# Elementwise products moved from POOL to VectorE, column blocks side by side, and gate weights loaded early, in a two-block layer stack

## The chip, the cores and the metric

The kernel runs on one core of a Trainium2 chip. The metric is device time in microseconds (us) of one launch; before the change the median of three runs is 3601.03 us (3599.94 to 3604.13). TensorE is called PE here, VectorE DVE, ScalarE ACT, GpSimd POOL and SyncE SP.

## What the reference computes

All arithmetic is float32, on 256 tokens of width 2048, batch 1. The first block has two layers. Layer 0 (`e_`) projects the normed input to 6144 columns; one half of the mixer is HGRN2, a gated linear recurrence in chunks, the other a causal convolution and an RG-LRU recurrence; both are gated and go through `e_w_out`. Layer 1 (`o_`) projects to 8208 columns: 2048 of q and k (convolution, SiLU), 2048 each of v, output gate and z, and 8 + 8 gate columns at the end (8192 to 8207) that make the decay of an mLSTM; then `o_w_out`. Each layer ends with

```python
h = h + mix
pl = rmsnorm(p[i] @ ple_w[i], ple_norm[i])
h = h + sigmoid(h @ ple_gate_w[i]) * pl
```

The second block has two equal layers: an SSD mixer beside a latent attention (MLA) from one projection of 3664 columns, joined by `w_out`; cross attention to a memory of 256 rows; a SwiGLU of width 5632 (`w_gate`, `w_up`, `w_down`). Every product with a weight is a matrix product of 256 tokens.

## The kernel before

**Dense products.** A weight is read once. `wload` (L204) brings a piece of 2 x 128 rows and up to 512 columns into one of four `raw` buffers by DMA on SP's queue, ACT rounds it to `whi` (L217), DVE makes the rest `wlo = raw - whi` (L218). An input is split the same way (`split`, L293), and a product is hi x hi + hi x lo + lo x hi. `tokens_chunks` (L238) makes a block of up to 512 output columns for all tokens in two accumulators (of five), piece by piece over the input's features; `cols_chunks` (L256) puts the output's columns on partitions and takes four. A piece of `tokens_chunks` is 12 matmuls.

**Order.** PE's order is written out by hand. `Flow` (L58) holds a queue `dense` of pieces, each with a condition (its input features exist), and a heap of generators for the side work. A generator yields the number of us of PE work that should pass before it goes on; `mm` (L138) counts that work. So `yield 6.5` in `hgrn_mix` places the next level's products 6.5 counted us later in PE's order. The order on DVE, ACT, POOL and SP is a scheduler's, from its own costs and priorities; each engine then runs its list in order. Weight pieces have a high priority.

**Where the change lies.** `hgrn_mix` (L602) runs seven levels for each of two halves: DVE makes `qd` (L618) and updates `sf` (L630), POOL makes `kd = k * sf` (L625) and updates `pf` (L634, its tile is called `sg` in the trace), PE multiplies `kd` and `qd`, DVE copies the result under a mask into `pa` and `pb` (L650). The mask keeps only the products that come from the first half of each pair of blocks of `m` columns. `lru_mix` (L723) multiplies `gi` by `xc` on POOL (L745) on the way to a scan; the scan's result, gated and split, is the last of the four feature blocks of `e_w_out`. `softmax` (L1111) ends with a scaling of each part on POOL (L1126), 32 times for `pu` of MLA and 16 times for `xp` of the cross attention. In the SSD mixer POOL makes `xdt` (L1411), scales `xtm` (L1414) and multiplies the decays `e` by `cbm` (L1435). The decays are made on DVE by L1426 and L1430.

`mix_out` (L799) makes a layer's output product in four column blocks, one after the other; with `halves=True` (the second block's `w_out`) the first two are taken side by side: half the pieces of block 0, half of block 1, the rest of 0, the rest of 1. `swiglu` (L1651) works through the 11 hidden blocks in groups of 3, 3, 3 and 2; after each group's gate and up products it makes four down blocks over the group's features. `bc_scores` (L1189) makes `cbm` 13 counted us after the convolution that gives `xbcc` was issued. The gate columns of `o_w_in` are loaded with 256 columns of v, as two DMAs for each of eight pieces (L210, L1059).

Of the kernel before, what the change touches and what calls it, by code (L numbers as in the profile page):

```python
# [20 lines left out]
KT = 16  # L21
# [71 lines left out]
def _body(tc, a, cst, msk, out):  # L93
# [3 lines left out]
    with ExitStack() as ctx:  # L97
# [103 lines left out]
            V.memset(mh, -0.5)  # L201


        def wload(w, k0, nk, *segs):  # L204
            with hp():
                nn = sum(n for _, n in segs)
                raw = raw_p.tile([128, 2, 512], F32, tag="raw", name="raw")[:, :nk, :nn]
                at = 0
                for n0, n in segs:
                    nc.sync.dma_start(  # L210
                        raw[:, :, at:at + n],
                        w[k0 * 128:(k0 + nk) * 128, n0:n0 + n].rearrange("(k p) n -> p k n", p=128),
                    )
                    at += n
                hi = hl_p.tile([128, 2, 512], F32R, tag="hi", name="whi")[:, :nk, :nn]
                lo = hl_p.tile([128, 2, 512], F32R, tag="lo", name="wlo")[:, :nk, :nn]
                S.activation(hi, raw, AF.Copy)  # L217
                V.tensor_tensor(lo, raw, hi.bitcast(F32), ALU.subtract)  # L218
            return [(k0 + j, hi[:, j, :], lo[:, j, :]) for j in range(nk)]
# [382 lines left out]
        def hgrn_mix(hf, st_):  # L602
# [10 lines left out]
            for n, m in enumerate(HGRN_LEVELS + (128,)):  # L613
# [7 lines left out]
                if m == 1:  # L621
                    kd = k
                elif m < 128:
                    kd = kds[n % 2]
                    G.tensor_tensor(kd, k, sf, ALU.mult)  # L625
                else:
                    kd = kds[n % 2]
                    V.tensor_tensor(kd[:, :, 0:128], k[:, :, 0:128], sf[:, :, 0:128], ALU.mult)
                if m < 128:
                    V.tensor_tensor(  # L630
                        halves(sf)[:, :, 0, :], halves(sf)[:, :, 0, :],
                        halves(pf)[:, :, 1, m - 1:m].to_broadcast([128, 512 // m, m]), ALU.mult,
                    )
                    G.tensor_tensor(  # L634
                        halves(pf)[:, :, 1, :], halves(pf)[:, :, 1, :],
                        halves(pf)[:, :, 0, m - 1:m].to_broadcast([128, 512 // m, m]), ALU.mult,
                    )
                    yield 6.5
                    sc = mx_tile([128, 4, 2, 64])
                    with hp():  # L640
                        for j in range(4):
                            for st in range(2):
                                mm(
                                    sc[:, j, st, :], kd[:, j, st * 128:(st + 1) * 128],
                                    qd[:, j * 128 + st * 64:j * 128 + (st + 1) * 64], start=True, stop=True,
                                )
                    mask = mk[:, n * 64:(n + 1) * 64].rearrange("p (b m) -> p b m", m=m)
                    for st in range(2):
                        dst = pa[:, :, 0:128] if st == 0 else pb
                        V.copy_predicated(  # L650
                            dst.rearrange("p j (b two m) -> p j b two m", two=2, m=m)[:, :, :, 1, :],
                            mask.unsqueeze(1).to_broadcast([128, 4, 64 // m, m]),
                            sc[:, :, st, :].rearrange("p j (b m) -> p j b m", m=m),
                        )
                else:
                    yield 6.0
                    sc = mx_tile([128, 4, 128])
                    with hp():
                        for j in range(4):
                            mm(sc[:, j, :], kd[:, j, 0:128], qd[:, j * 128:(j + 1) * 128], start=True, stop=True)  # L660
                    S.copy(pa[:, :, 128:256], sc)
# [61 lines left out]
        def lru_mix(hf, xb):  # L723
# [18 lines left out]
                        S.activation(dst[:, q, :], gp[:, j, :], AF.Sigmoid, bias=vc(bias, hf * 4 + q))  # L742
            for q in range(4):
                S.activation(th[:, q, :], th[:, q, :], AF.Tanh, scale=sp4[:, hf * 4 + q:hf * 4 + q + 1])
            G.tensor_tensor(gi, gi, xc, ALU.mult)  # L745
            rec = xb
            V.tensor_scalar(rec, th, 1.0, None, ALU.add)
            for q in range(4):
# [34 lines left out]
        def load_rest():  # L783
# [7 lines left out]
                yield from block2_cols(l)  # L791
            load(pos_i, a["positions_2"][0].rearrange("(m p) -> p m", p=128))

        def stat(st, key="ss"):
            if key not in st:
                st[key] = small([128, 2, 4], key)
            return st[key]

        def mix_out(yp, ks, w, gain, pairs, st=None, between=None, halves=False):  # L799
            def done(c):  # L800
                def go(ps):
                    res_add(ps, c)
# [3 lines left out]
            for c in range(4):  # L806
                if c == 2 and between is not None:
                    between()
                if halves and c == 0:
                    two = [tokens_chunks(done(n), reader(yp), ks, w, n * 512, 512) for n in range(2)]  # L810
                    half = len(two[0]) // 2
                    flow.dense.extend(two[0][:half] + two[1][:half] + two[0][half:] + two[1][half:])
                elif not halves or c > 1:
                    tokens_by_cols(done(c), reader(yp), ks, w, c * 512, 512)

        hgrn_values()
# [3 lines left out]
        for hf in range(2):  # L820
            hgrn_out(hf)
            lru_out(hf)

        def out_and_ple(i, yp, ks, w, after, hook=None):
            pairs, pl, made = [], [], []
            at(lambda: flow.spawn(made[0], 1.0))
            mix_out(yp, ks, w, None, pairs, between=lambda: made.append(ple(i, pl)))
            if hook is not None:
                at(hook)
            ple_gate(i, pairs, pl, after)  # L830
# [280 lines left out]
        def softmax(parts, scale, nm):  # L1111
# [11 lines left out]
                )  # L1123
            V.reciprocal(sums[:, :n], sums[:, :n])
            for i, (dst, _) in enumerate(parts):
                G.tensor_scalar(dst, dst, sums[:, i:i + 1], 0.0, ALU.mult, ALU.add)  # L1126


        def mixers(l, x, sx, yy):
# [57 lines left out]
                flow.spawn(bc_scores(conv_act(evac_rbc(ps, sx["rbc"], "xbc"), 2)))  # L1187

            def bc_scores(bc):  # L1189
                yield 13.0  # L1190
                cbm = b["cbm"] = unit([128, 2, 384], "cbm")
                for g in range(2):
                    sc = mx_tile([128, 384])
# [201 lines left out]
            def ssd_inputs(g):  # L1395
# [9 lines left out]
                for m in range(2):  # L1405
                    def per_head(ap):
# [1 line left out]

                    gs = slice(g * 8, g * 8 + 8)
                    xv = xtm[:, m, :].rearrange("p (a b) -> p a b", a=8)  # L1410
                    G.tensor_tensor(  # L1411
                        xdt[:, m, :].rearrange("p (a b) -> p a b", a=8), xv, per_head(b["dt"][:, m, gs]), ALU.mult
                    )
                    G.tensor_tensor(xv, xv, per_head(mixcol[l][:, 2, gs]), ALU.mult)  # L1414
                yssd[g], xdts[g] = xtm, xdt

            def ssd_decay(g, pr):
# [14 lines left out]
                        ALU.subtract, ALU.max,  # L1432
                    )
                S.activation(e, e, AF.Exp, scale=-1.0)
                G.tensor_tensor(e, e, b["cbm"][:, g, :].unsqueeze(1).to_broadcast([128, 2, 384]), ALU.mult)  # L1435

            def ssd_pair(g, pr):
                e = es.pop((g, pr))
# [212 lines left out]
        def swiglu(l, x, sx, x_next, s_next):  # L1651
            for c0, c1 in ((0, 3), (3, 6), (6, 9), (9, 11)):
# [29 lines left out]
                for c in range(c0, c1):  # L1682
                    cols_by_tokens(got_gate, reader(x), K16, a["w_gate_2"][l], c * 512)
                    cols_by_tokens(got_up(c), reader(x), K16, a["w_up_2"][l], c * 512)
                for c in range(4):
                    tokens_by_cols(
                        got_down(c), reader(acts), list(range(c0 * 4, c1 * 4)), a["w_down_2"][l], c * 512, 512
                    )

        xs, ss = x2, s2  # L1690
        for l in range(2):
            yy, x3, s3, oo, x4, s4, x5, s5 = [None] * 4, [], {}, [], [], {}, [], {}
            mixers(l, xs, ss, yy)
            mix_out(yy, K16[8:] + K16[:8], a["w_out_2"][l], lambda i, l=l: vc(f"xn{l}", i), x3, s3, halves=True)
            cross(l, x3, s3, oo)
            mix_out(oo, [0, 1, 2, 3], a["w_xo_2"][l], lambda i, l=l: vc(f"ffn{l}", i), x4, s4)
            swiglu(l, x4, s4, x5, s5)
# [30 lines left out]
```

## Time and profile before

| | before |
|---|---|
| median of 3 runs | 3601.03 us |
| profiled execution, span | 3601.81 us, 3600.0 us |
| PE busy | 3493.4 us (97%), 17927 matmuls |
| DVE busy | 2233.1 us (62%) |
| ACT busy | 1787.6 us (50%) |
| POOL busy | 180.9 us (5%) |
| HBM read | 624.92 MB, 174 GB/s over the span |
| mean granted clock of PE | 0.983 |

Durations come from one profiled execution. "Idle before" in a row is the time for which the engine stood still ahead of that group, and the arrow names what ended it. A granted clock of 1.00 is 2.4 GHz, 0.50 is 1.2 GHz.

### The profile page before, as it was taken

Reading aid. Unit: us, or ns where it says so; the run is one execution under the profiler, and the core shown is the slowest. Engines: PE = TensorE matmul, PEld = TensorE weight load, DVE = VectorE, ACT = ScalarE, POOL = GpSimd, SP = SyncE. Lnnn points to the kernel's source line nnn. Section 1 sums busy time; section 2 is a strip of 40 time slices with the busy share of each in tenths; the row PEclk is TensorE's granted clock in tenths of the full one; section 3 lists DMA queues with packets and bytes.
Section 4 is the critical chain, followed back from the end, with each engine's and each line's share of the span. In section 5 each row is a group of like instructions: output and inputs, shape, how many; then the busy total and the mean of one; then the engine's idle time right before and its main releaser. Section 6 shows DMA issues by size and latency. Waiting matters only on the chain.

```text
span 3600.0 us, 46977 instructions
## 1 busy us (share of the span) xinstructions
PE 3493.4 (97%) x17927; PEld 2976.8 (83%) x17927; DVE 2233.1 (62%) x3070; ACT 1787.6 (50%) x2626; POOL 180.9 (5%) x181
## 2 busy tenths in 40 slices
PE   9999898999999998999999999999989999999999
PEld 7888787888888877888888888898778888888887
DVE  5778756655567666556656555567666565555555
ACT  5344454544446545565444444455456654444443
POOL 0212000000000012000000000000110000000000
PEclk9999999999999999999999999999999999999999
DMA  7445468788666653546666666565436565666665
GB/s 222 146 141 173 158 183 142 190 177 173 206 199 174 180 147 109 196 154 183 193 187 187 192 187 190 175 182 167 128 118 201 156 189 192 187 191 188 187 189 163
DMA packets 338658, 630.14 MB, mean 175 GB/s; under 512 B 24416, under 2 KB 48128, under 8 KB 338432
## 3 DMA queue, kind: packets, MB, share of 16 engines
q1 hardware_dynamic: 335472, 621.86, 59.3%
q10 hardware_dynamic: 2960, 5.29, 0.5%
q8 instruction: 140, 2.29, 0.3%
q14 instruction: 86, 0.70, 0.1%
HBM read 624.92 MB, written 2.14 MB: 174 GB/s over the span
## 4 chain that ended last, share of the span: by engine, by line
PE 79%; DVE 2%; ACT 1%; issue 1%; DMA 0%; POOL 0%; ACTq 0%; POOLq 0%; DVEq 0%
PE acc L143 74%; PE mx L143 3%; PE tr L147 2%; DVE wlo L218 0%; ACT whi L217 0%; DVE e L1426 0%; DVE e L1430 0%; DVE xbcc L406 0%; ACT L1121 0%; ACT L1183 0%; ACT junk L326 0%; DMA lb<-lanes 0%; DVE thl L296 0%; ACT xbcc L1183 0%; ACT pu L1121 0%
## 5 line engine op out<-in xcount | busy, mean ns | idle before, releaser
L218 DVE TENSOR_TENSOR wlo<-raw,whi 128x1024 fp32r<-128x1024 f32 (+2 forms) x1184 | 1426.1, 1206 | 1180.3 <-ACT whi L217 1170.0
L217 ACT ACTIVATE whi<-raw 128x1024 fp32r<-128x1024 f32 (+2 forms) x1184 | 1232.9, 1042 | 1572.7 <-PE acc L143 1486.0
L143 PE MATMUL acc<-whi,thl 128*128 128x512 f32 (+4 forms) x5440 | 1688.4, 387 | 20.0 <-ACT thl L295 15.6
L143 PE MATMUL acc<-thl,whi 128*128 128x512 f32 x3968 | 1410.5, 400 | 13.8 <-ACT v L883 8.7
L143 PEld LDWEIGHTS acc<-whi,thl 128*128 128x128 f32 x5440 | 1022.1, 190 | 217.8 <-ACT thl L295 16.8
L143 PE MATMUL acc<-thl,wlo 128*128 128x256 f32 x3968 | 1116.5, 281 | 0.7 <-DVE wlo L218 0.7
L143 PE MATMUL acc<-wlo,thl 128*128 128x512 f32 (+4 forms) x2720 | 1045.0, 384 | 3.8 <-DVE wlo L218 3.7
L143 PEld LDWEIGHTS acc<-thl,whi 128*128 128x128 f32 x3968 | 748.7, 189 | 193.6 <-ACT v L883 9.0
L143 PEld LDWEIGHTS acc<-thl,wlo 128*128 128x128 f32 x3968 | 753.3, 190 | 1.7 <-DVE wlo L218 1.0
L143 PEld LDWEIGHTS acc<-wlo,thl 128*128 128x128 f32 x2720 | 516.2, 190 | 96.5 <-DVE wlo L218 5.5
L298 ACT ACTIVATE thl<-tr,vcols 128x256 fp32r<-128x256 f32 x216 | 92.4, 467 | 50.2 <-DVE thl L299 46.8
L299 DVE SCALAR_TENSOR_TENSOR thl<-tr,vcols,thl 128x256 fp32r<-128x256 f32 x216 | 96.4, 477 | 8.5 <-ACT thl L298 6.5
L331 POOL TENSOR_TENSOR r<-rsq,mh 128x2 f32<-128x2 f32 x11 | 7.7, 697 | 1500.7 <-DVE rsq L330 1500.7
L357 DVE TENSOR_TENSOR h<-acc,h 128x512 f32<-128x512 f32 x112 | 72.4, 681 | 8.2 <-PE acc L143 8.1
L326 ACT ACTIVATE junk<-h 128x512 bf16<-128x512 f32 x72 | 44.9, 624 | 7.8 <-DMA h<-in_x 3.8
L147 PE MATMUL tr<-cc,h 128*128 128x128 f32 x320 | 42.4, 276 | 0.0
L147 PEld LDWEIGHTS tr<-cc,h 128*128 128x128 f32 x320 | 38.1, 143 | 4.7
L367 ACT COPY gg<-acc 128x256 f32<-128x256 f32 x88 | 31.9, 363 | 11.8 <-PE acc L143 11.8
L367 ACT COPY uu<-acc 128x256 f32<-128x256 f32 x88 | 31.9, 363 | 11.8 <-PE acc L143 11.8
L143 PE MATMUL mx<-xdt,e 128*128 128x64 f32 x192 | 26.1, 291 | 7.9 <-DVE thl L296 7.9
L143 PEld LDWEIGHTS mx<-xdt,e 128*128 128x128 f32 x192 | 25.6, 209 | 9.6 <-issue 9.1
L368 DVE TENSOR_TENSOR uu<-acc,uu 128x256 f32<-128x256 f32 x88 | 32.9, 415 | 0.0
(393 smaller groups left out, 1757.7 us busy)
## 6 DMA issues: line engine op xcount, KB each, us to landing
raw<-in_w_gate SPq DMA_DIRECT2D x176, 512.0 KB
raw<-in_w_up SPq DMA_DIRECT2D x176, 512.0 KB
raw<-in_w_down SPq DMA_DIRECT2D x176, 512.0 KB
raw<-in_o_w_in SPq DMA_DIRECT2D x120, 512.0 KB
raw<-in_e_w_in SPq DMA_DIRECT2D x96, 512.0 KB
raw<-in_w_in SPq DMA_DIRECT2D x80, 512.0 KB
raw<-in_ple_gate_w SPq DMA_DIRECT2D x64, 512.0 KB
raw<-in_w_out SPq DMA_DIRECT2D x64, 512.0 KB
```

The costliest lines, as they stand in the source:

```text
L143: PE.matmul(o, lhsT, rhs, start=start, stop=stop)
L147: PE.transpose(o, x, eye)
L217: S.activation(hi, raw, AF.Copy)
L218: V.tensor_tensor(lo, raw, hi.bitcast(F32), ALU.subtract)
L298: S.activation(hi, src, AF.Copy, scale=gain)
L299: V.scalar_tensor_tensor(lo, src, gain, hi.bitcast(F32), ALU.mult, ALU.subtract)
L326: S.activation(junk[:, :n], src, AF.Square, accum_out=dst)
L331: G.tensor_tensor(dst, tmp[:, :n], mh[:, :n], ALU.pow)
L357: V.tensor_tensor(hs, ps[m], hs, ALU.add)
L367: S.copy(u[:, q, :], ps[q][:, 0])
L368: V.tensor_tensor(u[:, q, :], ps[q][:, 1], u[:, q, :], ALU.add)
```

## The change

Products on POOL become DVE instructions; `kd` is made only for the half that the mask keeps from the third level (m = 8) on. `mix_out` takes `parts` in place of `halves`: with `(4, 6)` blocks 0 and 1 go side by side in runs of four, two and two pieces. It now holds for `e_w_out` and `o_w_out` too, and `swiglu` puts its first two down blocks side by side, all but the last two pieces of each first. The 16 gate columns are loaded by one DMA into `gw`, a tile of the `w` pool, ahead of `e_w_out`; `wload` copies them from there on DVE. Two yields change.

```diff
 def wload(w, k0, nk, *segs):
 ...
             for n0, n in segs:
+                if n0 in kept:
+                    V.tensor_copy(raw[:, :, at:at + n], kept[n0][:, k0:k0 + nk, :])
+                    at += n
+                    continue
                 nc.sync.dma_start(
 ...
 # hgrn_mix
-                    G.tensor_tensor(kd, k, sf, ALU.mult)
+                    if n < 3:
+                        V.tensor_tensor(kd, k, sf, ALU.mult)
+                    else:
+                        V.tensor_tensor(
+                            halves(kd)[:, :, 0, :], halves(k)[:, :, 0, :], halves(sf)[:, :, 0, :], ALU.mult
+                        )
 ...
-                    G.tensor_tensor(
+                    V.tensor_tensor(
                         halves(pf)[:, :, 1, :], halves(pf)[:, :, 1, :],
                         halves(pf)[:, :, 0, m - 1:m].to_broadcast([128, 512 // m, m]), ALU.mult,
                     )
-                    yield 6.5
+                    yield 7.0
 # lru_mix
-            G.tensor_tensor(gi, gi, xc, ALU.mult)
+            V.tensor_tensor(gi, gi, xc, ALU.mult)
 ...
+        def side_by_side(jobs, parts):
+            for i, j in zip((0,) + parts, parts + (len(jobs[0]),)):
+                for job in jobs:
+                    flow.dense.extend(job[i:j])
 # mix_out
-                if halves and c == 0:
-                    two = [tokens_chunks(done(n), reader(yp), ks, w, n * 512, 512) for n in range(2)]
-                    half = len(two[0]) // 2
-                    flow.dense.extend(two[0][:half] + two[1][:half] + two[0][half:] + two[1][half:])
-                elif not halves or c > 1:
+                if parts and c == 0:
+                    side_by_side([tokens_chunks(done(n), reader(yp), ks, w, n * 512, 512) for n in range(2)], parts)
+                elif not parts or c > 1:
                     tokens_by_cols(done(c), reader(yp), ks, w, c * 512, 512)
 ...
+        def keep_gates():
+            kept[8192] = wtile([128, KT, 16], "gw")
+            load(kept[8192], a["o_w_in"][0][:, 8192:8208].rearrange("(k p) n -> p k n", p=128))
 # out_and_ple
+            if i == 0:
+                at(keep_gates)
-            mix_out(yp, ks, w, None, pairs, between=lambda: made.append(ple(i, pl)))
+            mix_out(yp, ks, w, None, pairs, between=lambda: made.append(ple(i, pl)), parts=(4, 6))
 # softmax
-                G.tensor_scalar(dst, dst, sums[:, i:i + 1], 0.0, ALU.mult, ALU.add)
+                V.tensor_scalar(dst, dst, sums[:, i:i + 1], 0.0, ALU.mult, ALU.add)
 # bc_scores
-                yield 13.0
+                yield 20.0
 # ssd_inputs, ssd_decay: xdt (L1411), xtm (L1414) and e (L1435)
-                    G.tensor_tensor(
+                    V.tensor_tensor(
 ...
 # swiglu
-                for c in range(4):
-                    tokens_by_cols(
-                        got_down(c), reader(acts), list(range(c0 * 4, c1 * 4)), a["w_down_2"][l], c * 512, 512
-                    )
+                down = [
+                    tokens_chunks(got_down(c), reader(acts), list(range(c0 * 4, c1 * 4)), a["w_down_2"][l], c * 512, 512)
+                    for c in range(4)
+                ]
+                side_by_side(down[:2], (len(down[0]) - 2,))
+                for job in down[2:]:
+                    flow.dense.extend(job)
 # the second block's w_out
-            mix_out(yy, K16[8:] + K16[:8], a["w_out_2"][l], lambda i, l=l: vc(f"xn{l}", i), x3, s3, halves=True)
+            mix_out(yy, K16[8:] + K16[:8], a["w_out_2"][l], lambda i, l=l: vc(f"xn{l}", i), x3, s3, parts=(4, 6))
```

## Rows read from the trace of the kernel before

**Rows 1.** PE's waits by releaser: total us, times, longest.

```profile
PE tr L147 <- POOL pu L1126: 17.3, 2, 8.7
PE acc L143 <- ACT thl L295: 15.6, 3, 11.4
PE mx L143 <- ACT xbcc L1183: 10.4, 2, 5.2
PE acc L143 <- ACT v L883: 8.7, 1, 8.7
PE mx L143 <- DVE thl L296: 7.9, 2, 4.0
PE tr L147 <- DVE thl L296: 7.4, 2, 3.7
...
PE mx L143 <- POOL kd L625: 5.0, 1, 5.0
...
PE acc L143 <- DVE xb L368: 4.7, 1, 4.7
```

**Rows 2.** Stretches: length, busy us of PE, PEld, DVE, ACT, POOL, clock, DMA, GB/s.

```profile
135.72:142.55 6.83, 5.21 (x16) 4.45 (x17) 6.83 (x12) 1.06 (x1) 1.15 (x1) 0.50 0.36 96
367.83:381.48 13.65, 5.03 (x11) 3.54 (x12) 8.56 (x10) 1.71 (x2) 0.00 (x0) 0.50 0.31 111
599.94:606.76 6.82, 3.33 (x10) 2.84 (x11) 3.25 (x4) 5.57 (x7) 0.00 (x0) 0.50 1.03 178
1238.23:1241.64 3.41, 3.14 (x10) 2.78 (x11) 0.00 (x0) 0.87 (x3) 0.00 (x0) 0.50 0.75 252
1333.80:1344.04 10.24, 3.96 (x11) 3.00 (x12) 6.05 (x12) 5.49 (x16) 8.61 (x10) 0.50 0.34 102
1412.31:1429.37 17.06, 11.33 (x37) 9.42 (x38) 8.96 (x17) 5.46 (x10) 4.05 (x3) 0.50 0.18 61
2327.08:2333.91 6.83, 6.56 (x15) 4.70 (x16) 1.44 (x2) 0.62 (x1) 0.00 (x0) 0.50 0.31 103
```

**Rows 3.** Single DVE lines: ns least, median, most; first and last start; form.

```profile
L1491 DVE TENSOR_TENSOR xtm<-xtm,zs x8: 682/688/692, 1394.8 to 2673.0; 128x512 f32<-128x512 f32 x8
...
L369 DVE TENSOR_TENSOR gg<-gg,rbc x22: 1224/1224/1226, 1653.6 to 3528.2; 128x1024 f32<-128x1024 f32 x22
...
L1333 DVE TENSOR_SCALAR kn<-kn,ckn x32: 272/278/281, 1277.1 to 2509.5; 128x128 f32<-128x128 f32 x32
```

**Rows 4.** DVE's groups over the span: busy us, mean ns, idle before.

```profile
L1426 DVE SCALAR_TENSOR_TENSOR e<-lb,acum,cc 128x256 f32<-128x256 f32 x32 | 27.9, 871 | 0.2
L618 DVE TENSOR_TENSOR qd<-q,sg 128x512 f32<-128x512 f32 x16 | 26.1, 1634 | 6.7 <-POOL sg L634 6.7
L1430 DVE SCALAR_TENSOR_TENSOR e<-lb,acum,cc 128x128 f32<-128x128 f32 x32 | 22.0, 689 | 0.0
```

**Rows 5.** The same view of the HGRN stretch, 100 to 320 us.

```profile
L218 DVE TENSOR_TENSOR wlo<-raw,whi 128x1024 fp32r<-128x1024 f32 x60 | 78.3, 1313 | 22.6 <-ACT whi L217 22.4
```

**Rows 6.** DVE in order of time: start, us; in HGRN, and ahead of `pu`.

```profile
131.86 2.84 DVE L618 TENSOR_TENSOR qd<-q,sg 128x512 f32<-128x512 f32 x1 [1.17 <-POOL sg L634]
...
1335.10 0.47 DVE L1426 SCALAR_TENSOR_TENSOR e<-lb,acum,cc 128x256 f32<-128x256 f32 x1
1335.49 0.34 DVE L1430 SCALAR_TENSOR_TENSOR e<-lb,acum,cc 128x128 f32<-128x128 f32 x1
...
1337.60 1.88 DVE L1430 SCALAR_TENSOR_TENSOR e<-lb,acum,cc 128x128 f32<-128x128 f32 x1
```

**Rows 7.** Stretches while `o_w_in` is read, columns as in rows 2.

```profile
540.00:562.00 22.00, 22.00 (x111) 18.63 (x110) 13.93 (x20) 12.48 (x18) 0.70 (x1) 1.00 0.92 179
562.00:586.00 24.00, 24.00 (x157) 22.10 (x156) 15.95 (x35) 10.10 (x18) 0.00 (x0) 1.00 0.95 91
612.00:632.00 20.00, 20.00 (x132) 18.04 (x131) 12.82 (x31) 6.90 (x14) 3.45 (x16) 1.00 0.42 103
640.00:680.00 40.00, 39.88 (x194) 33.42 (x193) 24.82 (x30) 20.39 (x24) 0.00 (x0) 0.96 0.75 222
```

**Rows 8.** A piece of the chain that ended last, in `w_out`: start, us, count.

```profile
1465.02 10.91 PE acc L143 x48
```

More of the change, by code (lines that the diff above doesn't have):

```diff
@@ L201, in _body @@
             V.memset(mh, -0.5)
+        kept = {}
         def wload(w, k0, nk, *segs):
@@ L797, in stat, with mix_out @@
             return st[key]
-        def mix_out(yp, ks, w, gain, pairs, st=None, between=None, halves=False):
+        def mix_out(yp, ks, w, gain, pairs, st=None, between=None, parts=()):
             def done(c):
@@ L1410, in ssd_inputs @@
                     xv = xtm[:, m, :].rearrange("p (a b) -> p a b", a=8)
-                    G.tensor_tensor(
+                    V.tensor_tensor(
                         xdt[:, m, :].rearrange("p (a b) -> p a b", a=8), xv, per_head(b["dt"][:, m, gs]), ALU.mult
                     )
-                    G.tensor_tensor(xv, xv, per_head(mixcol[l][:, 2, gs]), ALU.mult)
+                    V.tensor_tensor(xv, xv, per_head(mixcol[l][:, 2, gs]), ALU.mult)
                 yssd[g], xdts[g] = xtm, xdt
@@ L1434, in ssd_decay @@
                 S.activation(e, e, AF.Exp, scale=-1.0)
-                G.tensor_tensor(e, e, b["cbm"][:, g, :].unsqueeze(1).to_broadcast([128, 2, 384]), ALU.mult)
+                V.tensor_tensor(e, e, b["cbm"][:, g, :].unsqueeze(1).to_broadcast([128, 2, 384]), ALU.mult)
             def ssd_pair(g, pr):
```

## The prediction

> **What bounds the kernel now.** TensorE (PE) is busy for 3493.4 of 3600.0 us, so all that can be won by covering waits is the 106.6 us in which it is idle, and what it loses just after. The first view to read is therefore the list of PE's waits [rows 1]. It gives nearly all of the idle time, and the reader is to see that no single wait is large: POOL's scaling of `pu` 17.3, a split `thl` on ScalarE (ACT) 15.6, `xbcc` 10.4, the copy `v` 8.7, splits `thl` on VectorE (DVE) 7.9 and 7.4, `kd` on POOL 5.0, `xb` 4.7. The second view is the stretches in which the granted clock was 0.50 [rows 2]: one follows each long wait, at 1.2 instead of 2.4 GHz, so half of PE's busy time in them is lost as well. Third come DVE's groups, since seven product lines move there [rows 3 to 6]; fourth the DMA share around the gate columns [rows 7]; last the pace of PE, 10.91 us for four pieces of 12 matmuls, 2.73 us each [rows 8], which prices all work put in front of a wait.
>
> **The change part by part.** Terms are us, measured against the profiled execution (3601.81 with a span of 3600.0; the median of the runs is 3601.03, 0.8 lower).
>
> *Products to DVE.* Prices: 0.69 for 128x512, 1.22 for 128x1024, 0.28 for a 128x128 scaling [rows 3]; a scaling of 128x256 about 0.41 and a 128x768 product about 0.95 (estimates between these rows). Moved: `kd` 4 whole (1.22) and 8 halved (0.69) = 10.4; `pf` 14 x 0.69 = 9.7; `gi` 2 x 1.22 = 2.4; `xdt` and `xtm` 16 x 0.69 = 11.0; `e` 16 x 0.95 = 15.2; `pu` 16 x 0.28 + 16 x 0.41 = 11.0; `xp` 16 x 0.41 = 6.6. Together 66.
>
> Against that, DVE is now held up while POOL runs. `qd`, also 128x512, averages 1.634 where a free product takes 0.69: 16 x 0.94 = 15.1. `e` at L1426 averages 0.871 against 0.47 in a free row, at L1430 0.689 against 0.34, 32 each: 12.8 + 11.2 [rows 4, 6]. `wlo` averages 1.313 in the HGRN stretch against 1.22: 60 x 0.09 = 5.6 [rows 3, 5]. Returned: 45. DVE gains 66 - 45 = 21 us of work over the span, where it is busy 62% (table); in the HGRN stretch it gains 22.5 - 20.7, about 2. So DVE does not become the bound.
>
> What it does to the waits: (a) `xb` 4.7: the add that frees the accumulator was queued behind a `qd` of 2.84 [rows 6], which becomes 0.69, 2.2 earlier. At least 2.2 of 4.7 goes; if DVE's order also brings the add ahead of `wlo`, all, with 2.6 of half speed (half of 5.21 [rows 2]). I take 5. Bounds 2 to 7. (b) `kd` 5.0: this product waits for a buffer that L755 frees; `gi` puts 1.2 into the path to L755, the product itself gets shorter by about as much (its POOL form has no row here; 1.22 for 128x1024 on DVE), and two yields of 7.0 for 6.5 give PE 1.0 more work. I take 1.5; bounds -1 to 6. (c) `pu` 17.3, 8.7 in each layer: in DVE's order the reciprocal stands behind eight `e` instructions, of which the last took 1.88 for 0.34 [rows 6]. Freed, they are done some 3.0 earlier (4 x 0.40 + 4 x 0.35 by the means of [rows 4]); but `xdt`, `xtm` and `e`'s product, 4 x 0.69 + 0.95 = 3.7, may now come ahead of `pu`. So 0 if they do, and at most the whole wait and the half speed after it, 8.7 + half of 3.96. I take 3 each, nearest to the `e` that leave: 6; bounds 0 to 21. (d) the splits at L296, 7.9 + 7.4 in both layers: DVE is full there; 8 x 0.40 + 8 x 0.35 = 6.0 of held-up `e` leave and 4 x 0.95 + 4 x 0.69 = 6.6 of products arrive. I take 4 for the better order; below nothing is possible, since all in one queue can put `thl` later still. Bounds -4 to 26 (15.3 and, in each layer, half of 11.33).
>
> *bc_scores, yield 13 to 20.* PE comes 7.0 later to products that wait 5.2 for `xbcc` in each layer. The `q` projection's pieces stand in between. 2 x (5.2 + half of 3.14) = 13.5; DVE gets the evacuations of that work earlier too, so I take 12.5. Bounds 9 to 13.5. Nothing asks for `cbm` earlier: the steps that read it also wait for `krT`, which is later.
>
> *Two blocks side by side.* In e_w_out the longest `thl` wait, 11.4, is for the last feature block. Blocks 0 and 1 now put 12 pieces in front of it instead of 6: 6 x 2.73 = 16.4 > 11.4. But the chain before `thl` runs on DVE, and the `wlo` of those pieces now run among it (about four, 4.9) and `gi` adds 1.2: 16.4 - 6.1 = 10.3 of cover. With half of 5.03 at half speed, 13.9 at best; I take 11, bounds 6 to 14. In the last down group of each layer two pieces more (5.5) stand before the split that is waited for: 15.6 - 11.4 = 4.2 goes whole, and half of 6.56 with it in the first layer, about half of that in the second: 9; I take 8, bounds 6 to 9. The other down groups already have four pieces there and show no wait. The layers' own w_out and the second e-type block show none of size: 0. Accumulators: two blocks hold 4 of 5, and block 0 ends two pieces, 5.5, before block 2 wants its two; each `res_add` is 2 x 0.69. Hidden; without that cover it would cost 1.4 a time.
>
> *Gate columns ahead.* Around the gate projection the DMA engines are 95% busy for 91 GB/s; a piece of 272 KB then needs 2.9 us at full share, against PE's 1.45 (272 of 512 columns of 2.73). PE runs dry, and ACT, in whose order the late `whi` stand before the copy `v`, makes it wait 8.7. Without the 16-column loads the price of a 256 KB piece lies between 1.07 (612:632, 103 GB/s at 0.42) and 2.7 (no help); just before, 179 GB/s at 0.92 makes it 1.35 [rows 7]. That stretch reads the same tensor and is the nearest: 1.35, under PE's pace. So 8.7 + 1.7 of half speed = 10.4; I take 9, bounds 1 to 11. Eight copies of 32 elements on DVE are about 1.4, beside idle time. The load itself, 2048 runs of 64 bytes on SP's queue ahead of e_w_out: between 0 and 12.4 us of DMA time (8 x (2.9 - 1.35)). There the DMA share is 0.31 [rows 2] and four `raw` buffers hold 10.9 us of PE work: I take 0, at most 1.5. The buffer `gw` leaves five of six `w` tiles to the `sg` pairs until the gates: nothing.
>
> Sum: 5 + 1.5 + 6 + 4 + 12.5 + 11 + 8 + 9 = 57. 3601.8 - 57 = 3544.8; by the median, **3544**.
>
> The Trainium skill has a rule that speaks against the gate edit ("DMA: Bandwidth & Descriptors", How a descriptor splits into AXI transactions): a read that does not start on a 256-byte boundary fetches from the boundary below and pays for it. By it the rows of `o_w_in`, 32832 bytes apart (8208 columns of 4), are nearly all badly placed, with or without the gate columns, and the slowness stays (the first of the rivals). The trace agrees in part: 92% busy before any gate load, but 222 GB/s at 0.75 later in the same tensor [rows 7].
>
> **The rivals.** *DMA stays slow.* If `o_w_in` is slow by itself, a gate piece still needs 2.7, the wait stays, and 9 becomes 1: 3552. For: 0.92 before the gates. Against: 612:632, the same tensor in pieces of the same length.
> *DVE's order opens up.* With no product of POOL to wait for, (c) and (d) give 21 and 20 instead of 6 and 4: 3544 - 31 = 3513. For: POOL is named in the 17.3 and stretches the `e` before the splits. Against: DVE stays full there.
> *DVE becomes the bound, slower.* If the 45 us are not returned because DVE's order, and not POOL, sets them, the 59 us moved into HGRN (22.5) and SSD (37.2) push `wlo` back, and PE waits for it. Then (a) to (d) give nothing, 40 remain of the other edits, and the time is 3601 - 40 + 59 = 3620. It decides from 40/59, about two thirds of each moved us reaching PE. Against: a `qd` of 2.84 beside POOL's `kd` has the shape of the products that take 0.69, so what holds it lies outside DVE's queue [rows 3, 6].
> *The change does not do what it says.* The extra pieces sit behind the same late split (accumulators or `wlo` not free), and the gates still wait: only bc_scores and a part of the products remain, against new waits of their size: 3598.
>
> **How the numbers follow.** The forecast 60%, own range 3528 to 3562; slow DMA 15%; open order 13%; DVE the bound 7%; nothing 5%. Best terms of all parts would reach some 3490, worst 3582; at 8 in 10, 3512 to 3582. About 0.2%, 7 us, is what a measurement can tell from no change: faster 0.88, same 0.05, slower 0.07.
>
> **What would show it.** Right: `qd` at one length near 0.69, L1426 near 0.47; no wait of PE for `xbcc`, for `v` L883, for `thl` L295; the stretches at 0.50 after them gone; the DMA share at the gates well under 0.95 per byte moved. Wrong: PE waiting for `wlo` or for products on DVE by more than 10 us in all; the `v` wait still near 8.7; a new wait at the start of e_w_out.

## The result and the profile after

The changed kernel takes 3548.37 us (median of four runs, 3547.19 to 3551.89), against 3601.75 for the kernel before beside it: ratio 0.9853 with an interval of 0.9836 to 0.987. Run once more on another occasion it took 3550.40 (e11, below) against 3599.64, ratio 0.9861 [0.9848, 0.9875]. So it is 49 to 53 us faster. The forecast was 3544 with a range of 3512 to 3582.

Busy time of the engines after the change, part 1 of the page:

```profile
PE 3469.5 (98%) x17927; PEld 2961.9 (84%) x17927; DVE 2240.2 (63%) x3186; ACT 1786.8 (50%) x2626; POOL 53.2 (1%) x73
```

PE's 3469.5 of a span of 3545.7 leaves 76 us idle where it was 107. The other part of the gain is PE's busy time itself, 24 us less. Some 20 of them are what the half-speed stretches gave back: PE was busy for 77.5 us in stretches at 0.50 before and for 37.8 after, and half of the difference is 20. DVE took in 63 us of products (by their rows) and is busy 7.1 us longer.

PE's waits by releaser after the change (total us, times, longest), to set beside [rows 1]. Lines moved a little: L302 is the old L296, L903 the old L883, L1203 the old L1183, L1146 the old L1126, L632 the old L625.

```profile
PE tr L147 <- DVE pu L1146: 14.6, 2, 7.3
PE mx L143 <- DVE kd L632: 11.0, 1, 11.0
PE mx L143 <- DVE thl L302: 10.8, 2, 5.4
PE acc L143 <- ACT v L903: 8.7, 1, 8.7
...
PE tr L147 <- ACT xp L1141: 3.8, 2, 1.9
...
PE mx L143 <- ACT xbcc L1203: 1.6, 2, 0.8
PE tr L147 <- DVE xp L1146: 1.5, 2, 0.7
```

Three rows of before are gone: the ACT `thl` of 15.6, the `xb` of 4.7 and the second DVE row of `thl` (7.4); the first grew from 7.9 to 10.8. `xbcc` fell from 10.4 to 1.6. Two things the forecast did not have: `kd` grew from 5.0 to 11.0, and `v` did not move at all, which one of its rivals had.

DVE's groups, with the columns of [rows 4] (busy us, mean ns, idle before):

```profile
L1446 DVE SCALAR_TENSOR_TENSOR e<-lb,acum,cc 128x256 f32<-128x256 f32 x32 | 15.2, 476 | 0.0
L1455 DVE TENSOR_TENSOR e<-e,cbm 128x768 f32<-128x768 f32 x16 | 15.0, 946 | 0.0
L1450 DVE SCALAR_TENSOR_TENSOR e<-lb,acum,cc 128x128 f32<-128x128 f32 x32 | 11.0, 343 | 0.0
L624 DVE TENSOR_TENSOR qd<-q,sg 128x512 f32<-128x512 f32 x16 | 11.0, 685 | 0.1
...
L1146 DVE TENSOR_SCALAR pu<-pu,mas 128x256 f32<-128x256 f32 x16 | 5.5, 345 | 0.0
```

`qd` went from a mean of 1634 ns to 685, the two `e` forms from 871 and 689 to 476 and 343 [rows 4]: they now take what a row free of POOL took before [rows 6]. The Trainium skill states the mechanism ("SBUF — State Buffer", SBUF: two separate sides): a VectorE operation with two SBUF inputs and a GpSimd operation that reads SBUF exclude each other for a whole instruction. The traces agree: 2.84 us for a `qd` beside POOL [rows 6], 0.68 to 0.69 for every one of the 16 after. Two of the runs below show that it is the products on POOL: with all of them back there (e2) `qd` is slow again, and with only those of the SSD and the softmax back (e7) `e` is slow again, while `qd` stays at 689 ns. The row of e2, then that of e7:

```profile
L624 DVE TENSOR_TENSOR qd<-q,sg 128x512 f32<-128x512 f32 x16 | 26.1, 1633 | 6.7 <-POOL sg L640 6.7
```

```profile
L1446 DVE SCALAR_TENSOR_TENSOR e<-lb,acum,cc 128x256 f32<-128x256 f32 x32 | 27.9, 872 | 0.2
```

### The profile page after: what moved, and what is told of

Same layout as the page of the kernel before. It is cut to its first block, busy times and chain, and to the rows that moved or that the text cites. A ratio compares the mean times of both kernels' runs of the same rounds, so it can differ in the third digit from the quotient of the medians.

```text
span 3545.7 us, 46904 instructions
## 1 busy us (share of the span) xinstructions
PE 3469.5 (98%) x17927; PEld 2961.9 (84%) x17927; DVE 2240.2 (63%) x3186; ACT 1786.8 (50%) x2626; POOL 53.2 (1%) x73
## 4 chain that ended last, share of the span: by engine, by line
PE 79%; DVE 3%; ACT 1%; issue 1%; DMA 0%; POOL 0%; ACTq 0%; DVEq 0%
PE acc L143 74%; PE mx L143 3%; PE tr L147 2%; DVE wlo L224 1%; ACT whi L223 0%; DVE xbcc L412 0%; DVE e L1446 0%; DVE e L1450 0%; DVE e L1455 0%; DMA lb<-lanes 0%; ACT L1203 0%; DVE xdt L1431 0%; DVE qn L1250 0%; ACT xbcc L1203 0%; ACT pu L1141 0%
## 5 line engine op out<-in xcount | busy, mean ns | idle before, releaser
L143 PE MATMUL mx<-qd,kd 128*128 128x64 f32 (+1 forms) x208 | 26.6, 283 | 11.0 <-DVE kd L632 11.0
L143 PE MATMUL mx<-xdt,e 128*128 128x64 f32 x192 | 26.1, 291 | 10.8 <-DVE thl L302 10.8
L143 PEld LDWEIGHTS mx<-qd,kd 128*128 128x128 f32 x208 | 26.1, 202 | 12.1 <-DVE kd L632 11.5
```

The lines of the kernel that those rows point to most:

```text
L143: PE.matmul(o, lhsT, rhs, start=start, stop=stop)
```

## The experiments

Each ran beside the kernel before on the same chip. Repeats of one kernel spread over 2 to 9 us, so differences below 3 us are told by waits and stretches, not by medians. A stage mark is the end of a stage's last residual addition on DVE, counted from the span's start; the first closes layer 0, the second layer 1.

**e1, the moved products alone.** The kernel before with all seven product lines on DVE and the yield of 7.0, nothing else.

```diff
-                    G.tensor_tensor(kd, k, sf, ALU.mult)
+                    if n < 3:
+                        V.tensor_tensor(kd, k, sf, ALU.mult)
...
-                    yield 6.5
+                    yield 7.0
```

> The kernel before with only the seven product lines moved to DVE (kd halved from level three on, the HGRN yield at 7.0); down and output blocks, bc_scores and gate loads as before. Theory: the order edits cover waits that the products do not touch, so this alone is worth little: the xb wait (4.7 and its half speed) goes, the kd wait grows as in the changed kernel, the pu and L296 waits of the SSD stretches shrink by a third; 3585 to 3597 us, with PE still waiting 11 for thl at e_w_out and 5 twice for xbcc. Rival: freeing DVE from POOL carries the change; then 3565 or less, and the thl and xbcc waits shrink too.

Measured 3591.92, ratio 0.9985 [0.9975, 0.9994]: 6.6 us faster than before (3598.49 in these runs). Its waits:

```profile
PE acc L143 <- ACT thl L295: 16.7, 3, 12.5
PE tr L147 <- DVE pu L1131: 14.6, 2, 7.3
PE mx L143 <- DVE kd L626: 11.0, 1, 11.0
...
PE mx L143 <- ACT xbcc L1188: 10.4, 2, 5.2
```

`pu` and `kd` already stand as in the full change, so these two belong to the products; `xbcc` and the ACT `thl` stand as before, so these two belong to the order.

**e2, the order alone.** The changed kernel with all products back on POOL.

```diff
-            V.tensor_tensor(gi, gi, xc, ALU.mult)
+            G.tensor_tensor(gi, gi, xc, ALU.mult)
... the other six lines likewise, yield 7.0 back to 6.5
```

> The changed kernel with all products back on POOL (kd whole, HGRN yield 6.5): side by side blocks, gate columns ahead and bc_scores at 20 stay. Theory: 14 at e_w_out, 13 at bc_scores and 9 at the last down groups are gained without the products: 3562 to 3570 us; pu, L296 and kd waits as in the kernel before (17, 15, 5). Rival: the covers only work because DVE is free of POOL; then thl or xbcc waits return and the time is over 3580.

Measured 3558.55, ratio 0.989 [0.9874, 0.9907]: 40 us faster than before, 3 us under the range of the theory. The waits of the products are those of before again:

```profile
PE tr L147 <- POOL pu L1141: 17.3, 2, 8.7
...
PE mx L143 <- POOL kd L631: 5.0, 1, 5.0
PE acc L143 <- DVE xb L374: 4.7, 1, 4.7
```

So three quarters to four fifths of the gain (40 of 49 to 53 us) is order: which piece PE does while something else is late. The products give 6.6 us alone and 10 to 13 on top of the order (ratio 0.989 here, 0.9853 and 0.9861 for the whole change). The rival "DVE becomes the bound" is out: e1 is not slower but faster.

**e3, the gates by DMA.** The changed kernel without the load ahead.

```diff
-            if i == 0:
-                at(keep_gates)
```

> The changed kernel without the load ahead: the 16 gate columns come by DMA with each piece, as before. Theory: o_w_in is slow there by itself, so the load ahead is worth nothing: within 3 us of the changed kernel (3546 to 3551), wait for v still 8.7, DMA share about 1.0. Rival: the 64-byte loads did cost and something else took the place of their wait; then 5 to 10 us slower than the changed kernel.

Measured 3547.87, ratio 0.9861 [0.9846, 0.9876], with the same wait for `v` (8.7): loading the gate columns ahead is worth nothing that the runs can tell.

**e4, other columns first.** The blocks of q and k are read from columns 512 and 1536 before 0 and 1024, which computes another function with the same work in the same order.

```diff
-            cols_by_tokens(got, reader(x1), K16, w_in1, c * 512)
+            cols_by_tokens(got, reader(x1), K16, w_in1, (c ^ 1) * 512)
```

> The changed kernel, but layer 1's q and k blocks read their neighbour's columns (512 for 0, 1536 for 1024 and the other way round), so it computes another function; same work, same order. Theory: a block of o_w_in is slow when it is the first to be read of its neighbourhood, wherever it starts: packets of 2048 B still take about 185 ns in the first block, the wait for v stays at 8 to 9 us, the time within 3 us of the changed kernel. Rival: the place decides, blocks that start at a multiple of 4096 bytes are slow and the others fast: then the first and third block take about 110 ns a packet, the wait for v falls under 3 us and the time is 6 to 10 us lower.

My theory fell. Measured 3544.04, ratio 0.9848 [0.9833, 0.9862], 3.8 us under e3, which ran beside it, without overlap of the runs (3540.7 to 3545.0 against 3547.3 to 3550.0), and the wait for `v` is 4.0. The rival had the packets right, but put the wait under 3 and the gain at 6 to 10 us. The queue rows of three 22 us stretches tell why (packets, MB, share of 16 engines). The changed kernel, first block of `o_w_in`, columns 0 to 511:

```profile
q1 hardware_dynamic: 1986, 3.84, 92.2%
```

e4, its first block, columns 512 to 1023, and later columns 0 to 511:

```profile
q1 hardware_dynamic: 2119, 4.08, 62.3%
...
q1 hardware_dynamic: 1895, 3.66, 91.2%
```

The share times 16 times 22 us over the packets is 163 ns, 103 ns and 169 ns a packet: columns 0 to 511 are slow wherever they come in the order, columns 512 to 1023 are fast even as the first read.

**e5, `v` on DVE.**

```diff
-                    S.activation(v0[:, m, 0, :], gps[m][:, 16:272], AF.Copy, scale=r[:, m:m + 1])
+                    V.tensor_scalar(v0[:, m, 0, :], gps[m][:, 16:272], r[:, m:m + 1], None, ALU.mult)
```

> The changed kernel (3548.4 us), but the first quarter of the mLSTM's values is scaled out of the gates' accumulators by VectorE in place of ScalarE. Theory: of the 8.7 us wait for `v`, the part behind ScalarE's in-order queue (VectorE writes `fb` of the same accumulators at 579.83 us, ScalarE's second `v` ends at 584.46 us) goes away and the DMA's part stays: the wait falls to 3 to 6 us, the time to 3542 to 3546 us. Rival: the weight packets pace this stretch wholly, so that TensorE waits as long for the next piece: wait for `v` shorter, waits for `wlo` or `whi` longer by as much, 3547 to 3550 us.

What it was to take away is seen in the changed kernel's ACT rows (start, us):

```profile
580.62 1.06 ACT L223 ACTIVATE whi<-raw 128x1024 fp32r<-128x1024 f32 x1 [2.10 <-DMA raw<-in_o_w_in]
581.69 1.28 ACT L955 ACT_TABLE_LOAD   x1
582.99 1.06 ACT L955 ACTIVATE qk<-qkc 128x1024 f32<-128x1024 f32 x1
583.95 0.82 ACT L903 ACTIVATE v<-acc,r 128x256 f32<-128x256 f32 x2
```

`v` stands behind a `whi` whose weights are late, a table load and the sigmoid of the block before. Measured 3546.42, ratio 0.9856 [0.9841, 0.9871]; its waits from 550 to 640 us:

```profile
PE acc L143 <- DVE wlo L224: 3.0, 3, 1.9
PE acc L143 <- DVE v L903: 2.9, 1, 2.9
PE mx L143 <- DVE lf L911: 2.2, 1, 2.2
```

In the changed kernel the same stretch has 8.7 for `v` and 3.6 for `wlo`. So 5.8 us of the wait went, a new one of 2.2 came, and half speed is as long as before, now three times 3.41 us (from 576.0, 599.9 and 617.0) instead of 10.24 at once. The wait fell as the theory says; the time lies between the two expectations, 2 to 4 us under the changed kernel, which runs on different occasions can't tell from none.

**e6, `kd` first.** The `kd` lines inside `with hp():`.

```diff
+                    with hp():
                         if n < 3:
                             V.tensor_tensor(kd, k, sf, ALU.mult)
```

> The changed kernel, but VectorE's six masked-key products of each half (`kd`) are put at the priority of the split weights. Theory: the 11.0 us wait for the first `kd` of half 1 comes from its place in VectorE's order, behind the LRU's scans (buffer free at 244.97 us, `kd` issued at 250.47 us); ahead of them the wait falls to 4 to 6 us, the stretch at half speed behind it shortens too, and the time is 3537 to 3544 us. Rival: VectorE's order is not what holds it (the products before it, `qd` and the scans themselves, have to run anyway): the wait moves to `th`, `gi` or `wlo`, 3547 to 3551 us.

DVE's order ahead of the first `kd` of half 1, in the changed kernel, and then in e6:

```profile
243.75 1.22 DVE L766 TENSOR_TENSOR th<-th,gi 128x1024 f32<-128x1024 f32 x1
244.89 1.23 DVE L224 TENSOR_TENSOR wlo<-raw,whi 128x1024 fp32r<-128x1024 f32 x1
246.02 2.19 DVE L718 SCALAR_TENSOR_TENSOR sf<-sf,hrs,g 128x128 f32<-128x128 f32 x8
248.12 2.44 DVE L769 TENSOR_TENSOR_SCAN xb<-xc,th 128x256 f32<-128x256 f32 x4
250.47 1.20 DVE L632 TENSOR_TENSOR kd<-k,sf 128x1024 f32<-128x1024 f32 x1
```

```profile
243.84 2.19 DVE L719 SCALAR_TENSOR_TENSOR sf<-sf,hrs,g 128x128 f32<-128x128 f32 x8
245.94 1.23 DVE L633 TENSOR_TENSOR kd<-k,sf 128x1024 f32<-128x1024 f32 x1
247.07 1.28 DVE L770 TENSOR_TENSOR_SCAN xb<-xc,th 128x256 f32<-128x256 f32 x2
```

Only the four scans were passed: the wait is 8.7 instead of 11.0, by just their 2.35 us (248.12 to 250.47). Measured 3547.14, ratio 0.9858 [0.9842, 0.9874]: against the changed kernel nothing that the medians can tell. The place in DVE's order is right as a cause, but the `wlo` and the eight L718 (L719 in e6) stayed ahead. The `wlo` has the same priority; the L718 stand under no `hp()`, and why the scheduler keeps them ahead the runs don't show. Half speed behind the wait (13.65 us) stayed. So the theory holds for a fifth of the wait.

**e7, SSD and softmax products on POOL.** The HGRN's and LRU's stay on DVE.

```diff
-                V.tensor_tensor(e, e, b["cbm"][:, g, :].unsqueeze(1).to_broadcast([128, 2, 384]), ALU.mult)
+                G.tensor_tensor(e, e, b["cbm"][:, g, :].unsqueeze(1).to_broadcast([128, 2, 384]), ALU.mult)
... `xdt`, `xtm` and the scaling of `pu` and `xp` likewise
```

> The changed kernel, but the SSD's three products and the softmax scaling go back to POOL; the HGRN's and LRU's stay on VectorE. Theory: before the mixers nothing moves; in each mixers stage the waits for `thl` behind a POOL product come back and the residual adds of the two mixers stages end 5 to 7 us later each, while cross attention gives back 1 to 2.6 us in each layer: 3555 to 3561 us. Rival: of the 10 us between the kernel with all products on POOL (3558.6 us) and the changed one, the HGRN's and LRU's half is what counts: 3547 to 3552 us.

Measured 3554.97, ratio 0.988 [0.9865, 0.9895], at the theory's lower end. By the stage marks the two mixers stages are 5.6 and 4.7 us longer than in the changed kernel, and cross attention gives back 0.9 and 2.5. The rows behind the second part, cross attention of layer 0, the changed kernel first, then e7:

```profile
PE tr L147 <- ACT xp L1141: 1.9, 1, 1.9
PE tr L147 <- DVE xp L1146: 0.7, 1, 0.7
```

```profile
PE tr L147 <- POOL xp L1146: 0.4, 1, 0.4
...
PE tr L147 <- ACT xp L1141: 0.3, 1, 0.3
```

The softmax scaling of `xp` was better off on POOL, which had little else to do there: the cross attention stage takes 109.1 to 109.3 us in all three profiles that have `xp` on POOL (before, e2, e7) and 110.1 to 113.1 in the others.

**e8, the scores of B and C at 13 us.** One line, `yield 20.0` back to `yield 13.0`, run beside the changed kernel.

```diff
             def bc_scores(bc):
-                yield 20.0
+                yield 13.0
```

> The changed kernel, but the scores of B and C are again spaced 13 us instead of 20 behind their convolution. Theory (a term of 12.5 us for the two mixers stages): the waits for `xbcc` go from 1.6 back to about 10 us and TensorE's clock falls behind them: 10 to 14 us slower than the changed kernel. Rival: with the SSD's products on VectorE too, the tile comes earlier or another wait overlaps: 2 to 6 us slower.

Measured 3561.65 against 3550.40 for the changed kernel: 11.3 us, ratio to before 0.9895 [0.9882, 0.9909], and the wait is back as in [rows 1]:

```profile
PE mx L143 <- ACT xbcc L1203: 10.4, 2, 5.2
```

**e12, output blocks one after the other** in `e_w_out` and `o_w_out`, by leaving `parts=(4, 6)` out of the call in `out_and_ple`.

```diff
-            mix_out(yp, ks, w, None, pairs, between=lambda: made.append(ple(i, pl)), parts=(4, 6))
+            mix_out(yp, ks, w, None, pairs, between=lambda: made.append(ple(i, pl)))
```

> The changed kernel, but the first two column blocks of `e_w_out` and `o_w_out` are again computed one after the other. Theory (a term of 11 us, all at `e_w_out`): the wait for the split LRU output (`thl`, 15.6 us before) comes back at the second group of k, with half speed behind it: 9 to 14 us slower than the changed kernel, nothing at `o_w_out`. Rival: the VectorE products bring the LRU's output earlier, so the old order has less to wait for: 3 to 8 us slower.

Measured 3564.15, 13.8 us over the changed kernel beside it, ratio to before 0.9901 [0.9888, 0.9915]. All of it is at `e_w_out` (first stage mark 13.3 us later), with this wait and 13.65 us at half speed behind it:

```profile
PE acc L143 <- ACT thl L301: 12.5, 1, 12.5
```

**e9, the halves swapped.** The mLSTM's half 1 first, with `v` of the gates' block from column 3328.

```diff
-                tokens_by_cols(got_gates, reader(x1), K16, w_in1, 8192, 16, (2048, 256))
+                tokens_by_cols(got_gates, reader(x1), K16, w_in1, 8192, 16, (3328, 256))
... and the loop over hf, the order of `mlstm_out` and of k in `o_w_out` turned
```

> The changed kernel with the mLSTM's two halves in the other order, so that the first blocks read from `o_w_in` start at columns 512, 3328 (256 columns, beside the gates) and 1536 in place of 0, 2048 and 1024. It computes the same function. Theory (the place in the row decides: blocks that start at a multiple of 1024 columns take 185 ns a packet, others 110): these three blocks at 100 to 115 ns, the wait for `v` at 2 to 4.5 us, 3539 to 3544 us. Rival (what e4 gained hangs on the two column blocks that it swapped, and the gates' block with 1024 byte packets stays at 185 ns wherever it starts): the wait at 4 us still but the stretch no shorter than in e4, 3544 to 3547 us.

Measured 3544.44, ratio 0.9852 [0.9838, 0.9867]. With the packets counted off to the blocks in the order of issue, the first three blocks have mean packet times of some 110, 60 (256 columns) and 110 ns, and the wait for `v` is 4.0, as the place rule says. It was 4.0 in e4 too, where the gates' block was a slow one (some 170 ns), so what is left of the wait does not hang on that block's packets. But the next block, 256 columns from 3072, took some 180 ns; PE met it with a wait of 3.8 for `wlo` and 6.83 us at half speed from 613.9 on. The packets bear the theory out, the time is the rival's.

**e10, three repairs together** beside the changed kernel (**e11**): `kd` first, `v` on DVE, half 1 first with value blocks from columns 3840, 3328, 2816 and 2304.

```diff
-        for hf in range(2):
+        for hf, parts in ((1, ((5, 2), (3, 2))), (0, ((1, 2), (0, 1)))):
             qk_part(hf)
-            if hf == 0:
-                tokens_by_cols(got_gates, reader(x1), K16, w_in1, 8192, 16, (2048, 256))
+            if hf == 1:
+                tokens_by_cols(got_gates, reader(x1), K16, w_in1, 8192, 16, (3840, 256))
             qk_part(2 + hf)
-            v_part(2 * hf)
-            v_part(2 * hf + 1, mlstm_mix(hf))
+            v_part(*parts[0])
+            v_part(*parts[1], mlstm_mix(hf))
```

> The changed kernel with three repairs together, same function: `kd` at the split weights' priority, the gates' `v` on VectorE, and the mLSTM's half 1 first with its value blocks started at columns 3840, 3328, 2816 and 2304 (none a multiple of 1024; the multiples left are 0, 1024 and the last 256 columns at 2048). Theory: wait for `kd` 8 to 9 us in place of 11.0, for `v` under 3 in place of 8.7, the first five blocks of `o_w_in` at 100 to 115 ns (64 for the 256-column one), and no half-speed stretch between 570 and 620 us: 3534 to 3541 us. Rival: gains of this size are given back by half-speed stretches that fall elsewhere: 3542 to 3547 us.

> The changed kernel itself, as a measure beside the three others of this call on one chip: 3545 to 3549 us by either theory; the half-speed stretches may differ by one or two of 3.4 us from its first profile, the waits above 5 us by under 0.5 us.

e10 measured 3537.31 (3535.15 to 3539.27), ratio 0.9827 [0.9813, 0.984]; e11 3550.40 (3547.06 to 3552.11). It beats the changed kernel by 13.1 us with no overlap of the runs, while e5, e6 and e9 (ratios 0.9852 to 0.9858) don't stand apart from it (0.9853 and 0.9861). Its value blocks start elsewhere than e9's, so it is not just their sum, and that part was not run by itself. The gain lies in layer 1: 12.7 us less than e11 between the first and second stage marks, against 2.4 before the first. So `kd` first can have no more than those 2.4. Of the single edits e4 shortens layer 1 by 7.9 us against the changed kernel's profile, e5 and e9 by 1.4 and 1.3. Its waits from 550 to 640 us are two:

```profile
PE acc L143 <- DVE v L904: 0.9, 1, 0.9
PE mx L143 <- DVE lf L912: 0.3, 1, 0.3
```

`kd` waits 8.7, as in e6. The stretch 565 to 625 us (length, busy us of PE, PEld, DVE, ACT, POOL, clock, DMA share, GB/s), one fence each for e11, e9 and e10:

```profile
565.00:625.00 60.00, 47.00 (x296) 41.87 (x295) 40.86 (x95) 26.27 (x39) 3.87 (x16) 0.91 0.72 156
```

```profile
565.00:625.00 60.00, 51.12 (x293) 45.22 (x292) 43.98 (x99) 29.50 (x44) 6.24 (x16) 0.89 0.84 176
```

```profile
565.00:625.00 60.00, 58.85 (x309) 49.87 (x308) 51.15 (x104) 34.10 (x45) 5.38 (x16) 1.00 0.85 208
```

e9 shortens PE's idle time here, but the clock stays at 0.89 (0.91 in the changed kernel); only in e10 is PE busy throughout and the clock 1.00. One part of the expectation failed: four of the first five blocks read at some 110 ns (70 for the 256-column one), but the fifth, columns 2816 to 3327, at some 190. It contains column 3072. So what marks a slow block is that it contains a multiple of 1024 columns, not that it starts there.

## Why the prediction was right, point by point

The forecast of 3544 is 4 to 6 us under the time. The terms, in us saved; "measured" is from the run that isolates the term, or from stage marks of the changed kernel's profile where none does:

| term | predicted | measured | from |
|---|---|---|---|
| (a) `xb` and (b) `kd` | 6.5 | 5 to 6 | first stage mark of e12 (4.8) and e1 (6.2) |
| (c) `pu` and (d) splits | 10 | 10.3 in the mixers, less 3.4 that `xp` lost: 7 | changed kernel against e7 by stage marks |
| bc_scores | 12.5 | 11.3 | e8 |
| `e_w_out` side by side | 11 | 13.8 | e12 |
| last down groups | 8 | 10.2 | stage marks, 5.8 and 4.4 |
| gate columns ahead | 9 | 0 | e3 |
| sum | 57 | 47 to 48 | 49.2 beside e11, 53.4 at first |

*Products to DVE.* The ground of this part held: the time that POOL held DVE up came back. The moved products sum to 63 by their rows (the 128x768 product 946 ns against an estimate of 950, `pu` 345 against 410), the copies of the gate columns to some 1.4, and DVE is busy only 7.1 longer: 57 returned where 45 were forecast. `qd` and the two `e` forms give 39 of it (16 x 0.95 + 32 x 0.395 + 32 x 0.346). (a) went whole: there is no `xb` row. (b) has the wrong sign: the wait rose by 6.0. Two steps failed. One is "the product itself gets shorter by about as much". I priced `kd` as one instruction in place of another and did not ask what would stand ahead of it on its new engine: on POOL it began as soon as its buffer was free, on DVE it stands in order behind `wlo`, eight L718 and four scans, 5.5 us between the end of `th` (244.97) and its start (250.47). e6 took the scans out of the way and gained just their length. The other step is that (a) and (b) were added as if each stood alone. PE's rows at the end of this wait, before and after:

```profile
253.43 2.82 PE L143 MATMUL mx<-qd,kd 128*128 128x64 f32 x12 [4.98 <-POOL kd L625]
```

```profile
251.73 2.61 PE L143 MATMUL mx<-qd,kd 128*128 128x64 f32 x11 [11.04 <-DVE kd L632]
```

PE begins to wait at 240.69 instead of 248.45, 7.8 us sooner, since `xb` (4.7) and the half speed behind it (half of 5.2) no longer hold it up, and goes on only 1.7 us sooner. So `kd` was not later than before, but most of what (a) gave was waited away at (b). Some 3 us more come back behind the wait, where PE is busy for 5.9 us at half speed instead of 12.0; that makes 4.8, an estimate from these rows, beside the 4.8 and 6.2 of the stage marks.

(c) came out at 2.7 of wait (17.3 to 14.6), near the lower bound, for the reason that the bound named. Ahead of `pu` in the changed kernel:

```profile
1309.50 0.15 DVE L1144 RECIPROCAL mas<-mas 128x2 f32<-128x2 f32 x1
...
1309.63 0.68 DVE L1434 TENSOR_TENSOR xtm<-xtm,mixcols 128x512 f32<-128x512 f32 x1
...
1310.31 0.67 DVE L1431 TENSOR_TENSOR xdt<-xtm,dt 128x512 f32<-128x512 f32 x1
1310.90 0.95 DVE L1455 TENSOR_TENSOR e<-e,cbm 128x768 f32<-128x768 f32 x1
1311.77 1.00 DVE L1146 TENSOR_SCALAR pu<-pu,mas 128x128 f32<-128x128 f32 x4
```

The reciprocal comes earlier (4.7 us after PE began to wait, 8.0 before), and then three moved products, 2.3 us, stand between it and `pu`. (d) gave 4.5 of wait (15.3 to 10.8), close to the 4. With 10.3 in the mixers together, the rival by which (c) and (d) give 41 is out. Left out altogether was `xp` in cross attention, priced as DVE work and not as a wait: it costs about 1.7 us a layer.

*bc_scores, `e_w_out`, last down groups.* These three carried the forecast and each came within 3 us, the working by "pieces in front of the wait, 2.73 us each" included; the down groups gave the top of their bounds and a little more. No run has the down groups alone, but the two feed forward stages take 738.0 to 738.1 and 735.3 to 735.4 us in every profile that has this edit, and 743.9 to 744.2 and 739.7 to 740.3 in the two that don't (before, e1).

*Gate columns.* The step that failed is the choice of 1.35 us for a 256 KB piece from the neighbouring stretches. The rival "DMA stays slow" is what happened: the wait for `v` is 8.7 as before, and 10.24 us at half speed follow it, in one piece (before, 6.83 us and another 3.41 from 640.9 on):

```profile
578.40:588.64 10.24, 4.18 (x13) 3.60 (x14) 5.34 (x8) 5.30 (x7) 0.00 (x0) 0.50 1.01 174
```

The DMA engines are busy throughout with no load of 64-byte runs left. It is the block of columns that is slow (e4, e9, e10), with or without the gates. I compared it with 612:632 [rows 7] as "the same tensor in pieces of the same length"; that stretch read columns 2304 to 2559, which hold no multiple of 1024. The rival's 3552 was so the better account of this edit; that the forecast lay as close is luck, since `e_w_out` and the down groups gave 5 us more than taken. The Trainium skill's rule on starts ("DMA: Bandwidth & Descriptors", How a descriptor splits into AXI transactions), which the prediction set beside this rival, does not separate the blocks: the rows of all of them lie 32832 bytes apart, and they take some 100 to 120 ns or 160 to 200. By that rule the spacing, 64 bytes past a multiple of 256, leaves three rows of four off a boundary, not nearly all; and `w_in`, whose rows lie 14656 bytes apart, also 64 past a multiple of 256, shows only the short length.

Of the marks set beforehand, `qd` and L1446 at one length, no ACT `thl`, hardly an `xbcc` came true. The one against, "the `v` wait still near 8.7", did too, for its own term, and products on DVE do make PE wait for more than 10 us (`kd` 11.0, and `pu` 14.6, which POOL had held before).

## What to carry to other kernels

Price a moved instruction by what stands ahead of it on its new engine at that moment, not by its length: `kd` got shorter and still began 5.5 us after its buffer was free, and `xp` lost an idle engine. Waits in a row are not separate terms: what one gives back can be waited away at the next, as 6 of 7.8 us were here. Work that is put in front of a wait is priced well by the pace of the pieces, and it gave more here (35 us in three edits) than unloading an engine (6.6 alone, 10 to 13 on top of the order). A wait that late weights stand behind can have more than one releaser: three repairs that could hardly be told from nothing one by one, with the value blocks also started elsewhere, gave 13 us together, once PE no longer ran dry in that stretch and its clock stayed at 1.00. How much the value blocks alone would give, the runs don't show.

## What the runs showed of the hardware

Packets of 2048 bytes from one tensor take two lengths by column, by their means over a block of 512 columns: some 100 to 120 ns in blocks of `o_w_in` that contain no multiple of 1024 columns (those from 512, 1536, 2304, 2560, 3328, 3584, 4608, 5632, 6656 and 7680), some 160 to 200 in those that do (from 0, 1024, 2816, 3072, 4096, 5120, 6144 and 7168), in any order of reading. The 256-column blocks, packets of 1024 bytes, show it too: some 60 to 70 ns from 2304, 3328 and 3840, 165 to 190 from 2048 and 3072. The typical packet is not slower: in the changed kernel the median of the 2048-byte packets is 84 ns in nearly all blocks of either kind, but a quarter to a third of a slow block's packets take over 200 ns, and 5 to 11% of a fast one's. The other large tensors show only the short length (some 90 to 116 ns in `e_w_in`, `w_gate` and `w_in`). Why, the runs don't tell: rows are 64 bytes past a multiple of 4096 apart, so that over many rows all blocks start at the same set of offsets.

A repeat of one kernel moved its half-speed stretches (10.24 us in one profile and 13.65 in the other at the SSD of layer 1, 3.41 and 6.83 in its cross attention) and its span with them (3545.7 and 3550.3), with the waits in front of them unchanged to 0.1 us. Differences of that size between single profiles are no effect of an edit.
